# A hybrid decoder trunk on one core: 28 of 76 projection groups as seven products of quarters

## The chip, the core and the metric

One core of a Trainium2 chip runs the whole program in one launch. The metric is device time in microseconds (us). TensorE (PE) multiplies matrices, VectorE (DVE) and ScalarE (ACT) do elementwise work, GpSimd (POOL) a few reductions across partitions, and SyncE (SP) issues most DMAs. "PEld" in the profile is TensorE's loading of a stationary operand.

## What is computed

Two layers. Each normalises its input, projects it to 7,696 columns, sends them through three branches (a gated convolution, stick-breaking attention, gated linear attention or GLA), multiplies each by a SiLU gate, and projects the 2,048 mixed columns back onto the residual. All arrays are float32; there are 512 tokens of width 2,048.

```python
h = rmsnorm(x, norm_g)
proj = h @ w_in                                   # 2048 x 7696
y_conv = cv_b * (conv3(cv_c * cv_h) + bias) * silu(cv_g)
q, k = rmsnorm(sb_q), rmsnorm(sb_k)               # 8 heads of 128
z = q @ k.T / sqrt(128); keep = log_sigmoid(-z)   # strictly causal
w = exp(log_sigmoid(z) + reverse_cumsum(keep) - keep)
y_sb = (w @ sb_v) * silu(sb_g)
y_gla = rmsnorm(gla(gl_q, gl_k, gl_v, decay)) * silu(gl_g)
x = x + concat(y_conv, y_sb, y_gla) @ w_out       # 2048 x 2048
```

## The kernel before

**Float32 by three products.** Every operand of a projection is split into a high and a low float16 part, scaled by powers of two; a product is the sum of high x high, high x low and low x high in PSUM. The input's parts lie transposed in SBUF (`xh`, `xl`: 16 blocks of 128 of the inner dimension by 512 tokens), and so, later, do the parts of the mix (`mh`, `ml`).

**Groups.** The projections are cut into 76 groups of 256 weight columns (GW), 38 a layer, listed in `specs` (L272 to L284): six for GLA (V twice, Q, K, gate twice), four for the first half of the convolution (H, C, gate, B), for each of four head pairs V, gate, Q and K, four for the other half of the convolution, eight for the output. A group comes in three forms:

- `project_cols` (L556): weights stationary, 512 tokens moving; 2 column blocks x 16 x 3 = 96 matmuls. For results wanted with tokens along the free dimension: the convolution, the gates, GLA's q and k.
- `project_toks` (L580): tokens stationary, 256 weight columns moving; 4 token blocks x 16 x 3 = 192 matmuls into two PSUM banks. For V, Q, K of the attention and the output.
- `project_by_token` (L593): the same matmuls, one token block after the other in banks of their own.

PSUM for these results is the pool `psp` with three banks.

**Weights.** `weights()` (L412) opens each group: it fetches the weights two groups ahead from DRAM (`fetch`, two halves on SP's queue) and prepares those one group ahead (`load`, with high priority). Preparation sums the squares of both halves on ScalarE (`wmax`, L319), adds across partitions on GpSimd (L329), makes a power of two of it on VectorE (`wscale`, L330 to L350), then per half the high part on ScalarE (`whi`, L392) and the low part on VectorE (`wlo`, L399). For the output's weights each pair of inner blocks has a scale of its own, since the eight pieces of the mix have different scales (`ratio`, `wparts`).

**Order.** After a start whose VectorE and ScalarE order is written out (L98 to L550), the scheduler orders the instructions of each engine by priority and a timing model; each engine then runs its own in order. GLA's work lies beside the first convolution and head pair 0, attention of a pair beside the next pair's projections: `attend` leaves four pieces in a list, and `go()` emits one behind each projection. In `scores` (L936) a chunk of attention is four ScalarE passes (absolute value, exponential, logarithm, and the positive part), two VectorE passes to combine them, the reverse running sums (L962), a subtraction (L965), an exponential, and the split for the transposing DMAs.

**The mix.** Each finished piece of a branch is scaled and split at once into `mh` and `ml` (`mixsplit`, L643). These tiles also lend space to GLA before their columns are due. At the end of a layer the output groups add the residual (`finish`, L1074); in layer 0 they leave the sum in `xt`, and `xprep` (L472) normalises and splits it for layer 1, one token block at a time during the last group.

## Time and profile before

| | us |
|---|---|
| median of 3 runs | 1742.88 |
| fastest and slowest run | 1742.62, 1743.02 |
| span of the profiled execution, first to last instruction | 1740.9 |
| busy TensorE, VectorE, ScalarE | 1726.8, 1068.9, 1090.0 |

The profile gives its one execution by its span; the runs' times include what lies around a span, about 2.0 us by the median. The rows in the prediction come from these views: the page (busy shares); the timeline (start, duration, engine, line, operation, tiles, shape, count); the chain of work that ended last (start, us, what); the table by stage; and the groups of instructions (line, engine, operation, tiles, shapes, count | busy us, mean ns of one | idle us before them and what ended it). Starts of neighbouring instructions are closer together than durations, since the engines overlap the end of one with the next.

### The profile page before, as it was taken

What the parts mean: (1) busy time and instruction counts of PE and PEld (TensorE: products, weight loads), DVE (VectorE), ACT (ScalarE), POOL (GpSimd) and SP (SyncE); (2) the same over time, 40 slices, a digit from 0 to 9 for tenths busy, and PEclk for the clock granted to TensorE, in tenths of its full rate; (3) what the DMA queues carried; (4) which work ended last, traced back from release to release, by engine and by line L of the source; (5) the groups of instructions that cost most, each with busy time, mean ns of one, the idle gap of its engine ahead of it and who ended that gap; (6) DMA issues with size and microseconds to landing.
All of it is one profiled execution on the core that took longest, in us unless ns stands there. A gap on an engine that the chain in (4) does not pass through costs nothing.

```text
span 1740.9 us, 30651 instructions
## 1 busy us (share of the span) xinstructions
PE 1726.8 (99%) x12846; PEld 1232.4 (71%) x12846; DVE 1068.9 (61%) x2015; ACT 1090.0 (63%) x1460; POOL 75.1 (4%) x104
## 2 busy tenths in 40 slices
PE   8999999999999999999999999999999999999999
PEld 6744556868787754788885455668686868448888
DVE  7556788657665747433474576976575666673431
ACT  7558577667575867455555684766767667663540
POOL 1000000000000000000010000000000000000000
PEclk9999999999999999999999999999999999999999
DMA  6333313335353545444463333133454444453531
GB/s 222 121 97 97 98 58 113 103 104 131 108 140 110 128 121 128 134 158 146 138 148 105 97 97 97 50 121 110 125 124 109 117 124 126 112 132 113 177 124 40
DMA packets 266121, 204.69 MB, mean 118 GB/s; under 512 B 93106, under 2 KB 265212, under 8 KB 265472
## 3 DMA queue, kind: packets, MB, share of 16 engines
q1 hardware_dynamic: 256976, 193.29, 39.0%
q10 hardware_dynamic: 9008, 9.45, 1.6%
q8 instruction: 100, 1.64, 0.4%
q14 instruction: 37, 0.30, 0.1%
HBM read 173.36 MB, written 8.39 MB: 104 GB/s over the span
## 4 chain that ended last, share of the span: by engine, by line
PE 48%; issue 7%; DVE 1%; DMA 1%; SPq 0%; POOL 0%; ACT 0%; POOLq 0%; DVEq 0%
PE psp L576 8%; PE psp L578 8%; PE psp L577 8%; PE psp L570 6%; PE psp L568 6%; PE psp L569 6%; PE psp L601 3%; PE psz L749 1%; PE psm L988 1%; PE psz L944 1%; PE psz L840 0%; DMA m<-raw 0%; DVE wl L399 0%; SPq L487 0%; DMA xs<-x 0%
## 5 line engine op out<-in xcount | busy, mean ns | idle before, releaser
L577 PE MATMUL psp<-wl,m 128*128 128x256 f16 x1664 | 454.0, 273 | 0.0
L578 PE MATMUL psp<-wh,m 128*128 128x256 f16 x1664 | 453.9, 273 | 0.0
L576 PE MATMUL psp<-wh,m 128*128 128x256 f16 x1664 | 453.8, 273 | 0.0
L399 DVE SCALAR_TENSOR_TENSOR wl<-st,ws,wh 128x2048 f16<-128x2048 f32 (+1 forms) x120 | 282.3, 2353 | 193.1 <-ACT wh L392 179.7
L392 ACT ACTIVATE wh<-st,ws 128x2048 f16<-128x2048 f32 (+1 forms) x118 | 236.3, 2003 | 202.6 <-PE psp L569 100.9
L319 ACT ACTIVATE junk<-st 128x2048 uint8<-128x2048 f32 (+1 forms) x150 | 285.5, 1903 | 7.6 <-DMA st<-in_w_out_dram 4.5
L577 PE MATMUL psp<-wl,x 128*128 128x256 f16 x768 | 209.5, 273 | 0.0
L578 PE MATMUL psp<-wh,x 128*128 128x256 f16 x768 | 209.5, 273 | 0.0
L576 PE MATMUL psp<-wh,x 128*128 128x256 f16 x768 | 209.4, 273 | 0.0
L570 PE MATMUL psp<-m,wl 128*128 128x512 f16 x512 | 194.4, 380 | 0.0
L568 PE MATMUL psp<-x,wh 128*128 128x512 f16 x512 | 194.4, 380 | 0.0
L569 PE MATMUL psp<-x,wh 128*128 128x512 f16 x512 | 194.4, 380 | 0.0
L569 PE MATMUL psp<-m,wh 128*128 128x512 f16 x512 | 194.4, 380 | 0.0
L568 PE MATMUL psp<-m,wh 128*128 128x512 f16 x512 | 194.4, 380 | 0.0
L570 PE MATMUL psp<-x,wl 128*128 128x512 f16 x512 | 194.3, 380 | 0.0
L570 PEld LDWEIGHTS <-wl 128*128 128x128 f16 x1024 | 100.1, 98 | 122.8 <-issue 3.7
L569 PEld LDWEIGHTS <-wh 128*128 128x128 f16 x1024 | 100.1, 98 | 117.5 <-issue 1.1
L568 PEld LDWEIGHTS <-wh 128*128 128x128 f16 x1024 | 100.1, 98 | 115.3 <-issue 0.5
L576 PEld LDWEIGHTS <-m 128*128 128x128 f16 x1664 | 162.7, 98 | 19.9 <-issue 0.7
L578 PEld LDWEIGHTS <-m 128*128 128x128 f16 x1664 | 162.6, 98 | 19.4 <-issue 0.5
L577 PEld LDWEIGHTS <-m 128*128 128x128 f16 x1664 | 162.6, 98 | 18.8
L392 ACT ACTIVATE wh<-st,wsr 128x512 f16<-128x512 f32 x128 | 81.6, 710 | 100.5 <-PE psp L578 74.4
(285 smaller groups left out, 2260.4 us busy)
## 6 DMA issues: line engine op xcount, KB each, us to landing
st<-in_w_in_dram SPq DMA_DIRECT2D x120, 1024.0 KB, 5.3
st<-in_w_out_dram SPq DMA_DIRECT2D x32, 1024.0 KB, 5.5
x<-in_x_dram SPq DMA_DIRECT2D x4, 1024.0 KB
qT<-in_x_dram ACTq DMA_DIRECT2D x8, 512.0 KB, 5.3
qT<-xs ACTq DMA_DIRECT2D x8, 512.0 KB
xs<-x SPq DMA_DIRECT2D x14, 256.0 KB, 4.5
out_dram<-kT SPq DMA_DIRECT2D x14, 256.0 KB, 3.7
th<-za SPq DMA_TRANSPOSE x64, 3.6
```

What stands on the lines that cost most here:

```text
L319: S.activation(junk(HK * n).rearrange("p (k n) -> p k n", k=HK), staged[i][h][:, :, :n], AF.Square, accum_out=peak[i][:, h:h + 1])
L392: lasthi[i] = S.activation(wh[:, ks, :n], staged[i][h][:, ks, :n], AF.Copy, scale=s_)
L399: V.scalar_tensor_tensor(wl[:, ks, :n], staged[i][h][:, ks, :n], s_, wh[:, ks, :n], ALU.mult, ALU.subtract)
L568: T.matmul(o, wh[:, kk, cs], xh[:, :, k, :], start=st_, stop=False)
L569: T.matmul(o, wh[:, kk, cs], xl[:, :, k, :], start=False, stop=False)
L570: T.matmul(o, wl[:, kk, cs], xh[:, :, k, :], start=False, stop=en)
L576: T.matmul(o, ah[:, t, k, :], wh[:, kk, :n], start=st_, stop=False, skip_group_check=True)
L577: T.matmul(o, ah[:, t, k, :], wl[:, kk, :n], start=False, stop=False, skip_group_check=True)
L578: T.matmul(o, al[:, t, k, :], wh[:, kk, :n], start=False, stop=en, skip_group_check=True)
L601: T.matmul(o[:, :n], a_[:, t, k, :], w[k // HK][part][:, k % HK, :n], start=i == 0 and k == 0, stop=i == 2 and k == KT - 1)
L749: T.matmul(o, src16[sb][a][:, ss], tgt16[tb][b][:, g0:g1].rearrange("p g h c -> p (g h c)"), start=i == 0, stop=i == 2)
L944: T.matmul(z[:, o:o + (t + 1) * P], qT[:, a_, t, hh, :], kT[:, b_, :t + 1, hh, :], start=i == 0 and o % 512 == 0, stop=False, skip_group_c ...
```

## The change

**Seven products.** A group can be computed as a product of 2 x 2 blocks: tokens in two halves, the inner dimension in two halves, the 256 weight columns in two halves of 128. Instead of eight products of such quarters there are seven, of sums and differences of the quarters, in the form that needs four sums on each side, formed in place. `SEVEN` says which groups: the gate and K of every head pair, H of the second convolution half, output groups 2 to 6; 14 a layer. The sums of the weights are made in `right` for each such group, those of the input once a layer (`x_sums`, right after its preparation), those of the mix once a layer (`mix_sums`, before the output). `seven` runs the products and combines results while they leave PSUM, through `Raw` (to an unscaled SBUF tile) or `Residual` (onto the residual).

**Weights' tiles.** Prepared weights now lie in tiles of a quarter of the inner dimension (six buffers, high and low part together); a normal group uses four, a seven group seven. Stage buffers go from three to four.

**Mix in DRAM.** Finished pieces go to a DRAM tile in float32 (`spill`), and come back during the second convolution half (`mix_load`), except the last four, which are written in place. All pieces get one scale, known after that half's gate; `mix_split` then splits eight pairs, into the same two tiles that held the input's parts. The scale per pair of the output's weights goes. GLA gets tiles of its own.

**Attention and SiLU.** The running sum adds two arrays in one scan, which removes L958 and L965 and turns L959 around. The gate drops two ScalarE passes and replaces one VectorE pass by a minimum.

```diff
+SEVEN = {"gla": (), "conv0": (), "sb": (1, 3), "conv1": (0,), "out": (2, 3, 4, 5, 6)}
...
-    stage = ctx.enter_context(tc.tile_pool(name="stage", bufs=3))
-    wpool = ctx.enter_context(tc.tile_pool(name="wpool", bufs=3))
-    big = ctx.enter_context(tc.tile_pool(name="big", bufs=4))
+    stage = ctx.enter_context(tc.tile_pool(name="stage", bufs=4))
+    wpool = ctx.enter_context(tc.tile_pool(name="wpool", bufs=6))
+    big = ctx.enter_context(tc.tile_pool(name="big", bufs=2))
...
+    def right(i):
+        a, b = (staged[i][0][:, :, c * P:(c + 1) * P] for c in range(2))
+        c, d = (staged[i][1][:, :, c * P:(c + 1) * P] for c in range(2))
+        def part(x):
+            w = wtile(i)
+            hi, lo = (w[:, h, :HK * P].rearrange("p (k n) -> p k n", n=P) for h in range(2))
+            his.setdefault(i, []).append(S.activation(hi, x, AF.Copy, scale=scales[i]))
+            V.scalar_tensor_tensor(lo, x, scales[i], hi, ALU.mult, ALU.subtract)
+        part(a)
+        V.tensor_tensor(b, b, d, ALU.add)
+        V.tensor_tensor(a, a, b, ALU.add)
+        part(a)
+        part(c)
+        V.tensor_tensor(c, c, a, ALU.add)
+        V.tensor_tensor(a, a, d, ALU.subtract)
+        part(a)
+        part(b)
+        part(d)
+        part(c)
...
+    def seven(left, by_cols, evict):
+        w, u = weights()
+        def product(o, n, start, stop):
+            x = left[n]
+            for t in range(1 if by_cols else 2):
+                for k in range(HK):
+                    for i, (xi, wi) in enumerate(((0, 0), (1, 0), (0, 1)) if by_cols else ((0, 0), (0, 1), (1, 0))):
+                        ww = w[n][:, wi, k * P:(k + 1) * P]
...
+                        if by_cols:
+                            T.matmul(o[:, :2 * P], ww, x[xi][:, k, :, :], start=first, stop=final,
+                                     skip_group_check=True)
+                        else:
+                            T.matmul(o[:, t * P:(t + 1) * P], x[xi][:, k, t, :], ww, start=first, stop=final,
+                                     skip_group_check=True)
...
+        ev = evict(u)
+        o1 = bank(psp, "p")
+        product(o1, 0, True, False)
+        with tc.high_priority():
+            s1 = tmp("s1")
+            S.activation(s1, o1[:, :2 * P], AF.Copy, scale=ev.unit)
+        o2 = bank(psp, "p")
+        product(o2, 1, True, True)
+        with tc.high_priority():
+            u2 = tmp("u2")
+            ev.add(u2, o2[:, :2 * P], s1)
+        product(o1, 2, False, True)
+        ev.first(o1[:, :2 * P])
+        o3 = bank(psp, "p")
+        product(o3, 3, True, True)
+        with tc.high_priority():
+            vv = tmp("vv")
+            ev.sub(vv, o3[:, :2 * P], u2)
+        o4 = bank(psp, "p")
+        product(o4, 4, True, False)
+        ev.last4(vv, o4[:, :2 * P])
+        product(o2, 5, True, True)
+        ev.plus(0, 1, o2[:, :2 * P], vv)
+        product(o4, 6, False, True)
+        ev.plus(1, 0, o4[:, :2 * P], u2)
...
+    def column_sums(pieces):
+        tt = V.tensor_tensor
+        for x11, x12, x21, x22 in pieces:
+            tt(x22, x21, x22, ALU.subtract)
+            tt(x21, x11, x21, ALU.subtract)
+            tt(x11, x22, x11, ALU.subtract)
+            tt(x12, x12, x11, ALU.add)
...
+        def mix_split(k, s_):
+            y = m32[k // HK][:, k % HK:k % HK + 2, :]
+            hi, lo = (a[:, k:k + 2].rearrange("p k t c -> p k (t c)") for a in mix)
+            S.activation(hi, y, AF.Copy, scale=s_)
+            V.scalar_tensor_tensor(lo, y, s_, hi, ALU.mult, ALU.subtract)
...
-                S.activation(y, ps[c], AF.Copy, scale=u)
                 a = wk([P, seq], "ga")
-                S.activation(a, y, AF.Abs)
+                S.activation(a, ps[c], AF.Exp, scale=nu)
+                V.tensor_scalar(a, a, 2.0 ** 62, None, ALU.min)
+                S.activation(a, a, AF.Ln, bias=1.0)
                 S.activation(a, a, AF.Exp, scale=-1.0)
-                S.activation(a, a, AF.Ln, bias=1.0)
-                V.scalar_tensor_tensor(a, y, 0.0, a, ALU.min, ALU.subtract)
-                S.activation(a, a, AF.Exp)
-                V.tensor_tensor(y, y, a, ALU.mult)
+                V.scalar_tensor_tensor(g[:, c, :], ps[c], u, a, ALU.mult, ALU.mult)
...
-                    V.scalar_tensor_tensor(w, w, -1.0, a, ALU.mult, ALU.subtract)
-                    V.scalar_tensor_tensor(a, z[:, :zw], zs, w, ALU.mult, ALU.subtract)
...
-                        V.tensor_tensor_scan(back, ones.to_broadcast([P, (t + 1) * P]), back, 0.0,
-                                             ALU.mult, ALU.add)
-                    V.tensor_tensor(w[:, :zw - 1], w[:, :zw - 1], a[:, 1:], ALU.subtract)
+                        V.tensor_tensor_scan(keep_, grow_, keep_, 0.0, ALU.add, ALU.add)
+                    V.scalar_tensor_tensor(w, z[:, :zw], zs, a, ALU.mult, ALU.subtract)
...
+        y = conv_in(1, go)
+        m32 = mix_load()
+        s_ = conv_out(1, y, go)
         while later:
             go()
+        LATE = (10, 11, 2, 3)
+        for k in (0, 4, 6, 8, 12, 14, 10, 2):
+            mix_split(k, s_)
+        if any(modes[cursor[0]:cursor[0] + NG]):
+            sums = mix_sums(s_)
```

`mix_sums` runs `column_sums` twice on 1,024-wide pieces and splits the four sums in eight 1,024-wide steps, ScalarE and VectorE each; `x_sums` does the same on two token blocks of each half, then transposes the parts by sixteen DMAs. `Residual` reads PSUM six times per group and adds in SBUF three times, all 256 wide; `Raw` reads PSUM five times on VectorE. Both also copy the first product out of PSUM on ScalarE, and `Raw` one finished quarter.

533 lines of the change are left out of this document (343 added, 190 removed).

## The prediction

> **What bounds the kernel now.** I first read the page: its head, the busy shares and the granted clock.
>
> ```profile
> span 1740.9 us, 30651 instructions
> PE 1726.8 (99%) x12846; PEld 1232.4 (71%) x12846; DVE 1068.9 (61%) x2015; ACT 1090.0 (63%) x1460; POOL 75.1 (4%) x104
> PEclk9999999999999999999999999999999999999999
> ```
>
> TensorE is busy from end to end at full clock; VectorE and ScalarE are busy six tenths of the time. Since ends of matmuls are modelled, I check the busy share by the distance between starts: rows of the timeline of TensorE, then of the chain of work that ended last.
>
> ```profile
> 1100.18 0.38 PE L568 MATMUL psp<-m,wh 128*128 128x512 f16 x1
> ...
> 1104.28 0.38 PE L569 MATMUL psp<-m,wh 128*128 128x512 f16 x1
> ...
> 1105.20 1.45 PE L749 MATMUL psz<-m 128*128 128x128 f16 x23
> 1106.48 0.38 PE L570 MATMUL psp<-m,wl 128*128 128x512 f16 x1
> ```
>
> ```profile
> 1319.50 0.65 PE psz L944 x3
> ...
> 1410.10 0.65 PE psz L944 x3
> ...
> 1716.33 20.97 PE psp L601 x192
> ```
>
> Between the first two rows lie 19 matmuls of 512 columns: (1104.28 - 1100.18) / 19 = 0.2158 us each. The 23 of 128 columns take (1106.48 - 1105.20) / 23 = 0.0557 us each. The last group has 192 of 256 columns in 20.97 us, 0.1092 us each. So the time of TensorE goes with the columns streamed, with nothing between. One head pair of the attention stage repeats every 1410.10 - 1319.50 = 90.6 us.
>
> The third view is the table by stage (window; its length, then busy time and count of PE, PEld, DVE, ACT, POOL, the clock, DMA share, GB/s).
>
> ```profile
> 0.00:50.00 50.00, 42.33 (x285) 32.19 (x286) 39.05 (x99) 38.93 (x48) 10.24 (x12) 1.00 0.61 200
> 50.00:159.00 109.00, 109.00 (x606) 58.28 (x605) 58.02 (x133) 65.59 (x77) 5.19 (x8) 1.00 0.36 113
> 159.00:255.00 96.00, 96.00 (x553) 48.81 (x551) 75.56 (x153) 64.77 (x105) 1.33 (x3) 1.00 0.24 77
> 255.00:350.00 95.00, 95.00 (x805) 74.81 (x804) 71.85 (x139) 65.69 (x96) 2.62 (x6) 1.00 0.35 106
> 441.00:532.00 91.00, 91.00 (x748) 71.62 (x746) 58.87 (x100) 62.98 (x77) 4.61 (x5) 1.00 0.45 119
> 712.00:754.00 42.00, 42.00 (x388) 37.63 (x387) 14.85 (x32) 15.72 (x32) 0.80 (x2) 1.00 0.35 115
> 754.00:859.00 105.00, 105.00 (x964) 94.00 (x963) 41.69 (x84) 58.21 (x106) 1.99 (x5) 1.00 0.52 164
> 859.00:908.00 49.00, 46.22 (x421) 41.08 (x420) 33.78 (x64) 30.34 (x44) 7.82 (x4) 1.00 0.55 126
> ```
>
> In every stage between the start and the change of layers TensorE leaves nothing idle, so taking columns away shortens each of them, until VectorE, the next engine in the GLA stage (79% and 76%), is full.
>
> **The columns removed.** A column-form group now has 96 matmuls of 512, 96 x 0.2158 = 20.72 us; as seven products it has 7 x 24 = 168 of 256, 168 x 0.1092 = 18.35 us: 2.37 less. A token-form group has 192 of 256, 20.97 us; as seven products 7 x 48 = 336 of 128, 336 x 0.0557 = 18.70 us: 2.27 less. Per layer the table SEVEN makes five column-form groups (four gates, the first of conv1) and nine token-form ones (four K, five of the output). 10 x 2.37 + 18 x 2.27 = **64.5 us** less on the engine that is full. No other matmul changes.
>
> **What it adds to VectorE and ScalarE.** Rows of the groups by line and shape, and of VectorE's timeline, where consecutive instructions overlap a little:
>
> ```profile
> L399 DVE SCALAR_TENSOR_TENSOR wl<-st,ws,wh 128x2048 f16<-128x2048 f32 x116 | 272.4, 2349 | 186.7 <-ACT wh L392 173.2 <-PE psz L946 10.2 <-PE psz L749 2.9
> L392 ACT ACTIVATE wh<-st,ws 128x2048 f16<-128x2048 f32 x114 | 227.9, 1999 | 196.9 <-PE psp L569 100.9 <-PE psp L578 73.9 <-DVE ws L340 9.6
> L1044 DVE TENSOR_TENSOR raw<-raw,qr 128x1024 f32<-128x1024 f32 x8 | 9.8, 1226 | 0.3
> L1053 ACT ACTIVATE qp<-raw 128x1024 f16<-128x1024 f32 x16 | 16.9, 1057 | 44.0 <-DVE raw L1049 25.8 <-DVE raw L1044 18.1
> L330 DVE TENSOR_SCALAR wq<-wgm 128x1 f32<-128x1 f32 x75 | 16.0, 213 | 141.4 <-POOL wgm L329 141.4
> L338 DVE TENSOR_SCALAR wq<-wq 128x1 int32<-128x1 int32 x76 | 11.4, 150 | 1.5
> L735 DVE TENSOR_TENSOR m<-e,m 128x256 f16<-128x256 f32 x32 | 13.4, 423 | 7.8 <-ACT m L734 7.3
> ```
>
> ```profile
> 1267.81 1.20 DVE L620 TENSOR_REDUCE bm<-g 128x1 f32<-128x1024 f32 x1
> 1268.92 2.34 DVE L399 SCALAR_TENSOR_TENSOR wl<-st,ws,wh 128x2048 f16<-128x2048 f32 x1
> 1271.18 1.55 DVE L965 TENSOR_TENSOR zw<-zw,za 128x895 f32<-128x895 f32 x2
> ...
> 1279.12 0.87 DVE L995 SCALAR_TENSOR_TENSOR e<-psm,vu,g 128x256 f32<-128x256 f32 x2
> ```
>
> L399 occupies 1271.18 - 1268.92 = 2.26 us of the engine, 0.09 less than its duration. So a 1024-wide operation costs 1.226 - 0.09 = 1.14 us, a 256-wide one from PSUM about 0.39 (two took 0.87), a 256-wide one in SBUF 0.423 - 0.09 = 0.33.
>
> Preparing a seven group: seven low parts and five sums or differences, each 1024 wide, 12 x 1.14 = 13.7 us of VectorE where two L399 took 4.5 (+9.2), and 7 x 1.06 = 7.4 us of ScalarE where two L392 took 4.0 (+3.4). Its results: five 256-wide operations on VectorE, 2.0 us; the output groups have six from PSUM and three in SBUF, 3.3 us.
>
> *Attention stage, one head pair.* The window 441 to 532 has 58.9 us of VectorE. Two seven groups add 2 x (9.2 + 2.0) = 22.4. Removed are L958, L965 and L648:
>
> ```profile
> L958 DVE SCALAR_TENSOR_TENSOR zw<-zw,za 128x896 f32<-128x896 f32 (+1 forms) x4 | 3.1, 823 | 5.2 <-ACT za L954 5.2
> L965 DVE TENSOR_TENSOR zw<-zw,za 128x895 f32<-128x895 f32 (+1 forms) x4 | 3.1, 812 | 0.0
> L648 DVE SCALAR_TENSOR_TENSOR m<-e,bsmix,m 128x512 f16<-128x512 f32 x2 | 1.5, 752 | 0.0
> L962 DVE TENSOR_TENSOR_SCAN za<-ones,za 128x512 f32<-128x512 f32 (+3 forms) x8 | 5.9, 805 | 0.0
> ```
>
> The first three make 3.1 + 3.1 + 1.5 less ten overlaps of 0.09, 6.8 us. New sum 58.9 + 22.4 - 6.8 = 74.5 us against TensorE's 90.6 - 2.37 - 2.27 = 86.0: 87% full. I cost the scan that adds two arrays like the scan with a constant, L962; the trace has no such scan, and if its second array halved its pace, VectorE would need 5.9 us more and still fit. ScalarE, by these rows:
>
> ```profile
> L611 ACT ACTIVATE g<-psp,wu 128x512 f32<-128x512 f32 x32 | 21.2, 670 | 0.0
> L613 ACT ACTIVATE ga<-g 128x512 f32<-128x512 f32 x32 | 20.0, 630 | 0.5
> L1033 ACT ACTIVATE raw<-psp 128x512 f32<-128x512 f32 x32 | 18.4, 576 | 0.0
> L647 ACT ACTIVATE m<-e,bsmix 128x512 f16<-128x512 f32 x16 | 11.5, 718 | 24.7 <-DVE e L995 24.7
> ```
>
> 63.0 + 2 x 3.4 + some 1.6 for copies of first results, less 2 x (0.67 + 0.63) for the passes that the shorter SiLU drops, 2 x 0.58 for K's raw copies and 2 x 0.72 for the mix: 66 us, 77%. The right-hand sums also make VectorE wait twice per group for a 1.06 us high part of a sum just formed, about 1.1 us each: 4.4 us a head pair, inside the 11.5 idle. So I charge 0 here. The bounds are 0 (other ready work always fills the waits) and 18 groups x 2.2 = 40 us (nothing does); I take 0 because the idle time is more than twice the waits.
>
> *GLA stage into the first head pair.* 75.6 + 71.9 = 147.4 us of VectorE in 191; plus 22.4, less some 4 of mix splits: 166 against 186, 89%. Also 0, inside the same bounds.
>
> *Output stage.* There is no attention work to fill waits. A seven group costs VectorE 13.7 + 3.3 + 0.8 (five scalars of the scale, L330 and four like L338) = 17.8 us against 18.70 of TensorE. With the two waits it is 20.0, so VectorE sets the pace: 1.3 us a group, x 10 = **+13 us**. Below, the bound is 0 (the scheduler pulls two independent high parts forward), above 2.2 x 10 = 22.
>
> *Between attention and output.* The mix is now split at the end: eight pairs at 1.14 = 9.1 us of VectorE, and its sums for the seven products, 8 x 1.14 + 8 x 1.14 = 18.2. The window 712 to 754 has 14.9 us in 42; there the preparation of the first seven group takes the place of eight narrow low parts,
>
> ```profile
> L399 DVE SCALAR_TENSOR_TENSOR wl<-st,wsr,wh 128x512 f16<-128x512 f32 x128 | 87.5, 747 | 40.3 <-ACT wh L392 40.0
> ```
>
> ```profile
> st<-in_w_in_dram SPq DMA_DIRECT2D x120, 1024.0 KB, 5.3
> ```
>
> 13.7 less 8 x 0.66, about 8 more (the second row is the page's, a weight half's fetch and its us to landing). Sum 50 us, in 42 plus what of the last conv group is free (the first half of K is readable there already for overwriting). So VectorE is full for two groups; TensorE needs the sums one product after the other, not at once. I charge 3 us a layer, **+6**; bounds 0 and 50 - 42 = 8 a layer. The twelve loads of the mix from DRAM, 3.1 MB, have about 60 us; with 6.3 MB of weights beside them that is about 155 GB/s, and the start moves 200. Hidden. If it were not, the split would wait, and the output stage with it.
>
> *Layer start.* Sums of the input: 16 x 1.14 = 18.2 us of VectorE and 16 more transposing DMAs, behind the input's preparation, where the window 0 to 50 has 39 of 50 busy and 50 to 159 58 of 109. Seven products don't read them for eleven groups, some 230 us. But if they stand ahead of the evictions of the first two groups, TensorE has three PSUM banks of 5.2 us each, 15.7 us, before it waits. 18.2 plus the low parts of one group, 4.5, less 15.7 is 7 us; the other end is 0. I charge 3 a layer, **+6**.
>
> Moved queues: stores of the mix, its loads and the input's transposes stand on SP before weight fetches. A load waiting for its buffer holds those fetches, but weights are fetched two groups, some 40 us, ahead; cost 0, and the latency of a weight fetch, 5.3 us by the last row above, each time that cover is gone.
>
> **Sum.** On the profiled execution: 1740.9 - 64.5 + 13 + 6 + 6 = 1701.4. The median of the runs is 1742.88, 2.0 above the span; carried along, the forecast is **1703**.
>
> **Rivals.**
>
> 1. *TensorE stays the only bound*: the waits are all filled. Then 1742.9 - 64.5 = 1678. For it: 39% of VectorE is idle before. Against it: it would need the output stage at 95% of VectorE without a bubble.
>
> 2. *Late evictions* (slower). A seven group uses four results in three PSUM banks. The fourth needs the bank of the first; the product that completes the fourth needs its half result read; the next group needs the bank of the second. Each has one product, 48 x 0.0557 = 2.7 us, as cover, and the reading instruction stands in VectorE's queue between the 1.14 us steps of the next weights. Two of these ahead make 2 x 1.14 + 0.39 = 2.7, no wait; three make 3.8, a wait of 1.1. If three stand there at all three places of all 28 groups, that is 3 x 1.1 x 28 = 92 us: 1742.9 - 64.5 + 92 = 1770. It decides above 64.5 / 28 = 2.3 us a group. For it: the engine is 87 to 95% full around these groups, and an engine that waits in order also delays what is behind. Against it: the evictions carry high priority, and two steps are still covered.
>
> 3. *Weight loads bind the 128-column stream.* Each load lasts 98 ns by its row:
>
> ```profile
> L749 PEld LDWEIGHTS <-m 128*128 128x128 f16 x432 | 30.4, 98 | 9.6
> ```
>
> If loads did not overlap one another, 336 x 0.098 = 32.9 us a token-form group instead of 20.97: 1742.9 - 23.7 + 18 x 12.0 = 1935. Against it stands the burst above, 23 loads and matmuls at 0.0557. The row has 432 loads of 98 ns, 42.3 us, in 30.4 us of busy time, so they overlap. The burst is short beside 336 in a row, which no row shows. The Trainium skill, page "TensorE: Matmul & The Clock Gate", section "Back-to-back issue gap", says that a sustained stream of weight load and matmul pairs runs at about 81 ns each at 128 columns. By that, an estimate, a token-form group would take 27.2 us and the kernel 1742.9 - 23.7 + 18 x 6.2 = 1831; the trace disagrees as far as its bursts reach, 55.7 ns.
>
> 4. *The saving is eaten exactly*: the bounds of the attention stage and the others together, 40 + 22 + 16 + 14 = 92, exceed 64.5, so a result near no change can come out, too.
>
> **Chances.** Forecast, some waits filled, 1690 to 1730: 0.50. Rival 1, below 1690: 0.17. More of the bounds, 1730 to 1739: 0.09. Within 0.2%, about what a measurement of this kernel can tell from no change: 0.04. Rival 2: 0.16. Rival 3: 0.04. So faster 0.76, same 0.04, slower 0.20. The range runs from 1680, where every added cost is nearly nothing, to 1748, which takes in rival 4 and the mild end of rival 2; 2 in 10 are left outside, most of it above.
>
> **What will show it.** Step one: matmuls of 128 columns start 56 ns apart in long runs, and TensorE has 64 us less work. Attention: a head pair of 86 us with VectorE near 75 busy; a longer one, with TensorE waiting for high or low weight parts or for PSUM, shows my 0 wrong. Output stage: seven groups of 20 us, VectorE without idle time but for waits on ScalarE's high parts. Mix: a pause of TensorE of about 3 us near the third output group. Start: waits of TensorE for evictions while VectorE forms sums. Rival 2 shows as TensorE's idle time before third and fourth results, put down to VectorE reading PSUM; rival 3 as starts over 80 ns apart without waits. The forecast is wrong if the seven groups last over 21 us, or if the sums take VectorE much longer than 1.14 us a step.

## The result, and the profile after

The changed kernel takes 1766.85 us (median of four runs, 1759.59 to 1770.10) against 1742.95 before on the same chip: 1.0132 times as long, 95% interval 1.0111 to 1.0154. It is slower by 24 us where 40 us less was forecast.

From the page of the kernel after, its head and busy shares, and from its view of cores the mean granted clock:

```profile
span 1768.3 us, 38034 instructions
PE 1694.0 (96%) x16158; PEld 1315.4 (74%) x16158; DVE 1361.6 (77%) x2417; ACT 1188.4 (67%) x1588; POOL 65.3 (4%) x104
...
core 0: 1768.3 us, clock 0.984
```

TensorE has less work and yet the span is longer: its share fell from 99 to 96%, VectorE's rose from 61 to 77%, and the mean clock, 1.00 in every window of before, is 0.984. Part of the 1694.0 is therefore matmuls that ran slowly. The table by stage (length, then busy us of PE, PEld, DVE, ACT, POOL, clock, DMA share, GB/s) says where:

```profile
18.00:63.00 45.00, 34.54 (x249) 28.22 (x249) 42.30 (x82) 32.80 (x44) 1.77 (x4) 0.89 0.51 131
428.00:459.00 31.00, 26.16 (x369) 23.81 (x368) 24.37 (x39) 19.33 (x24) 0.63 (x1) 0.89 0.68 183
459.00:522.00 63.00, 63.00 (x592) 55.84 (x590) 46.48 (x83) 47.31 (x62) 2.69 (x4) 1.00 0.36 91
458.47:554.35 95.88, 89.38 (x960) 79.70 (x958) 71.26 (x122) 66.64 (x86) 3.32 (x5) 0.96 0.50 119
777.00:875.00 98.00, 94.86 (x1682) 94.02 (x1680) 87.41 (x131) 70.37 (x105) 3.61 (x5) 1.00 0.57 180
949.00:984.00 35.00, 27.66 (x109) 11.28 (x107) 14.65 (x27) 14.66 (x19) 4.97 (x4) 0.85 0.75 172
```

Rows one, two and six are the start of layer 0, the group K of head pair 1, and the third group of layer 1: there TensorE idles and its clock is 0.85 to 0.89. Between them (row three, the V, gate and Q groups after that K) it is full at full clock. Row four is one head pair from V to V, row five five seven-product groups of the output.

To add such pauses up, one number is used from here on. The prediction's rows gave the distance between starts of matmuls in a full stream: 0.0557, 0.1092 and 0.2158 us for 128, 256 and 512 columns (and, from the trace of before, 0.1158 and 0.1625 for the few of 272 and 384). The **lost time** of a stretch is the sum over its matmuls of the distance to the next start, less that; it is worked out from the starts in a run's trace. It holds idle time and slow clock together. A group reaches from its first projection matmul to the next group's first, counted in the order of the program.

| lost us | starts of the two layers (six GLA groups each) | K of pairs 1 to 3 and the groups next to it | output | all |
|---|---|---|---|---|
| before | 7.8 | 0 | 0 | 7.5 |
| after | 33.5 | 47.5 | 11.4 | 95.8 |

The rest of the last column, 3.3 us after, lies beside GLA's matmuls in the gate of pair 0. The balance closes: 1740.9 - 64.5 (columns) + 95.8 - 7.5 = 1764.7, and 3.6 is left to the measured 1768.3, at the starts of the layers where other matmuls lie. So the saving is there in full, and 88 us of new pauses eat it.

**One pause at K.** TensorE's timeline after (start, duration, line, tiles, shape, count, idle before and what ended it). L665 are a seven group's products, L626 to L628 the V group that follows, L1199 attention beside them.

```profile
438.03 4.41 PE L665 MATMUL psp<-w,s 128*128 128x128 f16 x76
442.28 0.27 PE L1199 MATMUL psm<-th,v 128*128 128x256 f16 x1
443.86 1.31 PE L1199 MATMUL psm<-th,v 128*128 128x256 f16 x12 [1.31 <-DMA th<-za]
445.01 2.84 PE L665 MATMUL psp<-w,s 128*128 128x128 f16 x48
...
451.25 0.40 PE L626 MATMUL psp<-w,act 128*128 128x256 f16 x1 [3.02 <-DVE wq L356]
...
456.99 0.32 PE L626 MATMUL psp<-w,act 128*128 128x256 f16 x1
```

Three things are in these rows. A wait for transposed attention weights (1.3 us). A wait of 3.0 us before V's first matmul. And behind it 27 matmuls from 451.25 to 456.99, 0.213 us apart where 0.109 is the full pace: half clock, worth 2.8 us more. With a wait of 0.7 us for ScalarE's copy of the first result, ahead of these rows, they make the 8.2 us lost at this K. The Trainium skill, page "TensorE: Matmul & The Clock Gate", section "Part 1: The HAM clock gate", says that the clock falls to half after an idle window of about 3.4 us and knows no steps between; 0.213 against 0.109 agrees with the half, but the wait was 3.02 us, shorter than that window (the last section returns to it).

The second wait is the new one. VectorE's timeline of the same moment:

```profile
442.93 0.42 DVE L709 TENSOR_TENSOR vv<-psp,u 128x256 f32<-128x256 f32 x1
447.11 1.23 DVE L429 TENSOR_TENSOR st<-st,st 128x1024 f32<-128x1024 f32 x1 [3.76 <-DMA st<-in_w_in_dram]
448.25 1.28 DVE L412 SCALAR_TENSOR_TENSOR w<-st,ws,w 128x1024 f16<-128x1024 f32 x1
449.45 1.22 DVE L1266 SCALAR_TENSOR_TENSOR qp<-raw,qp 128x1024 f16<-128x1024 f32 x1
450.58 0.20 DVE L348 TENSOR_SCALAR wq<-wgm 128x1 f32<-128x1 f32 x1
450.77 0.42 DVE L721 TENSOR_TENSOR raw<-psp,vv 128x256 f32<-128x256 f32 x1
```

L721 reads the PSUM bank that V's first matmul needs. Its inputs were there when L709 ended, at 443.3. But VectorE works in order, and ahead of L721 the scheduler had put L429, the first sum of the weights of the gate group of pair 2, which starts at 477.7. L429 waited 3.76 us for those weights to land, and three more steps stood between: the eviction came 7.4 us late. (TensorE's wait is put down to L356, the instruction just behind L721.) Why had the weights not landed? SyncE's queue:

```profile
434.58 0.37 SPq L320 DMA_DIRECT2D st<-in_w_in_dram  x1
435.05 6.23 SPq L1181 DMA_TRANSPOSE th<-za  x3
441.37 0.53 SPq L320 DMA_DIRECT2D st<-in_w_in_dram  x1
```

The first half's fetch (L320) left at 434.58, the second half's only at 441.37, behind three transposes of attention, and L429, which needs both, could start at 447.1. That is still 30 us before the group that multiplies with these weights: they were late for the place of L429 in VectorE's queue, not for TensorE. A fetch also waits until a stage buffer comes free. The largest such wait, after and before (us in all, times, longest):

```profile
SPq L320 <- DVE w L412: 270.4, 30, 20.2
SPq L308 <- DVE wl L399: 975.6, 121, 20.5
```

It is longer before, where nothing is lost at K, so a sum of waits on this queue explains no pause.

L429 stands and waits like this at the K groups of pairs 1 and 2 in both layers, 3.8 to 5.5 us each time. At pair 3 it doesn't, and about 6.6 us are lost each time all the same: TensorE waits for transposed attention weights there, and for an eviction on ScalarE (L713) that stands behind a sum of squares (L332), which itself waited 1.9 us for a fetch.

**The start of layer 0.** VectorE, then TensorE:

```profile
35.65 1.23 DVE L749 TENSOR_TENSOR x<-x 128x1024 f32<-128x1024 f32 x1 [0.66 <-PE psz L498]
...
38.44 1.22 DVE L751 TENSOR_TENSOR x<-x,x 128x1024 f32<-128x1024 f32 x1
39.57 2.48 DVE L488 SCALAR_TENSOR_TENSOR x<-x,xrs,g 128x1024 f32<-128x1024 f32 x2
41.96 2.35 DVE L507 TENSOR_TENSOR act<-psz,act 128x1024 f16<-128x1024 f32 x2
...
43.32 1.94 PE L498 MATMUL psz<-ident,x 128*128 128x128 f32 x8 [5.50 <-DVE act L507]
...
57.14 7.07 PE L638 MATMUL psp<-w,act 128*128 128x272 f16 x47 [4.62 <-ACT w L408]
```

L749 to L751 are sums of the input that nothing reads for eleven groups; they stand ahead of L488 and L507, which prepare the input blocks that TensorE multiplies next.

**The third group of layer 1**, in the timelines of SyncE, ScalarE, VectorE and TensorE:

```profile
956.97 5.51 SPq L775 DMA_TRANSPOSE s<-th  x4
962.58 12.20 SPq L320 DMA_DIRECT2D st<-in_w_in_dram  x3
...
968.20 1.91 ACT L332 ACTIVATE junk<-st 128x2048 uint8<-128x2048 f32 x1 [12.53 <-DMA st<-in_w_in_dram]
...
970.81 0.21 DVE L348 TENSOR_SCALAR wq<-wgm 128x1 f32<-128x1 f32 x1 [14.55 <-POOL wgm L345]
971.13 0.67 DVE L847 COPY e<-psm 16x512 f32<-16x512 f32 x1
...
971.85 2.07 PE L851 MATMUL psm<-e,ga 16*128 16x512 f32 x2 [7.34 <-DVE ws L358]
```

The sixteen transposes of the input's sums (L775) take 5.51 / 4, about 1.4 us of the queue each, 22 us in all. The weight fetch behind them leaves at 962.58, the sum of squares that needs it (L332) waits 12.5 us, and the scale (L348) waits for that. TensorE doesn't need this scale for another 33 us: it is that of the group after next, which starts at 1004.3. What it waits for is the copy L847, which its matmul L851 reads, and L847 stands behind L348 in VectorE's queue. It is the same trap as at K, with another wait at its head. (TensorE's wait is put down to L358, the instruction just behind L847.)

### The profile page after: what moved, and what is told of

Its sections match the earlier page's. It is cut to its first block, busy times and chain, and to the rows that moved or that the text cites. A ratio compares the mean times of both kernels' runs of the same rounds, so it can differ in the third digit from the quotient of the medians.

```text
span 1768.3 us, 38034 instructions
## 1 busy us (share of the span) xinstructions
PE 1694.0 (96%) x16158; PEld 1315.4 (74%) x16158; DVE 1361.6 (77%) x2417; ACT 1188.4 (67%) x1588; POOL 65.3 (4%) x104
## 4 chain that ended last, share of the span: by engine, by line
PE 19%; DVE 14%; issue 12%; DMA 5%; ACT 5%; SPq 1%; POOL 1%; ACTq 0%; DVEq 0%; POOLq 0%
PE psp L665 5%; PE psp L638 2%; PE psp L662 2%; DMA st<-in_w_in_dram 2%; DVE w L412 2%; DVE w L426 2%; PE psp L626 2%; PE psp L628 2%; PE psp L627 2%; ACT junk L332 1%; PE psp L610 1%; PE psp L611 1%; PE psp L612 1%; DMA th<-za 1%; DVE za L1173 1%
## 5 line engine op out<-in xcount | busy, mean ns | idle before, releaser
L626 PE MATMUL psp<-w,act 128*128 128x256 f16 x1280 | 353.7, 276 | 14.9 <-DVE wq L356 11.7
L627 PE MATMUL psp<-w,act 128*128 128x256 f16 x1280 | 353.6, 276 | 0.8 <-DVE w L412 0.8
L628 PE MATMUL psp<-w,act 128*128 128x256 f16 x1280 | 353.2, 276 | 0.0
L332 ACT ACTIVATE junk<-st 128x2048 uint8<-128x2048 f32 x150 | 285.3, 1902 | 53.4 <-DMA st<-in_w_in_dram 52.0
L425 ACT ACTIVATE w<-st,ws 128x1024 f16<-128x1024 f32 x196 | 219.2, 1142 | 150.6 <-DVE st L430 35.4
L412 DVE SCALAR_TENSOR_TENSOR w<-st,ws,w 128x1024 f16<-128x1024 f32 x192 | 244.3, 1279 | 51.6 <-ACT w L408 50.7
L426 DVE SCALAR_TENSOR_TENSOR w<-st,ws,w 128x1024 f16<-128x1024 f32 x196 | 248.3, 1281 | 45.3 <-ACT w L425 43.9
L408 ACT ACTIVATE w<-st,ws 128x1024 f16<-128x1024 f32 x188 | 212.7, 1142 | 90.9 <-PE psp L612 60.0
L610 PE MATMUL psp<-act,w 128*128 128x512 f16 x704 | 268.0, 381 | 0.0
L611 PE MATMUL psp<-act,w 128*128 128x512 f16 x704 | 267.9, 380 | 0.0
L612 PE MATMUL psp<-act,w 128*128 128x512 f16 x704 | 267.7, 380 | 0.0
L662 PEld LDWEIGHTS <-w 128*128 128x128 f16 x1680 | 165.5, 99 | 26.8 <-issue 5.0
L665 PE MATMUL psp<-w,act 128*128 128x128 f16 x2592 | 152.5, 219 | 5.5 <-ACT s L676 4.3
L665 PEld LDWEIGHTS <-act 128*128 128x128 f16 x2592 | 147.4, 98 | 6.9 <-issue 6.4
L638 PE MATMUL psp<-w,act 128*128 128x256 f16 (+1 forms) x1152 | 137.7, 281 | 12.1 <-ACT w L408 5.3
L626 PEld LDWEIGHTS <-act 128*128 128x128 f16 x1280 | 126.9, 99 | 28.4 <-DVE wq L356 12.4
L627 PEld LDWEIGHTS <-act 128*128 128x128 f16 x1280 | 126.9, 99 | 20.0 <-issue 4.1
L628 PEld LDWEIGHTS <-act 128*128 128x128 f16 x1280 | 127.0, 99 | 17.6 <-issue 1.6
L638 PEld LDWEIGHTS <-act 128*128 128x128 f16 x1152 | 114.5, 100 | 33.1 <-issue 9.3
L610 PEld LDWEIGHTS <-w 128*128 128x128 f16 x704 | 69.1, 98 | 82.9 <-issue 3.8
L611 PEld LDWEIGHTS <-w 128*128 128x128 f16 x704 | 69.1, 98 | 82.5 <-issue 3.8
L612 PEld LDWEIGHTS <-w 128*128 128x128 f16 x704 | 69.1, 98 | 82.0 <-issue 2.0
```

The lines of the kernel that those rows point to most:

```text
L332: S.activation(junk(HK * GW).rearrange("p (k n) -> p k n", k=HK), staged[i][h], AF.Square, accum_out=peak[i][:, h:h + 1])
L412: V.scalar_tensor_tensor(lo[:, :, :GW], staged4(i, q), scales[i], hi[:, :, :GW], ALU.mult, ALU.subtract)
L425: his.setdefault(i, []).append(S.activation(hi, x, AF.Copy, scale=scales[i]))
L426: V.scalar_tensor_tensor(lo, x, scales[i], hi, ALU.mult, ALU.subtract)
L610: T.matmul(o, wh, xh[:, k, :, :], start=st_, stop=False)
L611: T.matmul(o, wh, xl[:, k, :, :], start=False, stop=False)
```

## The experiments

Theories, by the letters of the expectations (Q is their name for all these local waits together; B and V, rivals, are explained where they stand). **D**: at the K groups a wait for a weight fetch stands ahead of a pressing eviction. **O**: at the start of a layer the sums of the input stand ahead of the input's own preparation. **S**: the block of sixteen transposes holds up what is behind it on its queue. The rival **R**: the rest of the change (the mix in DRAM, the new tiles, the attention) costs the time, not the seven products.

### Which part

All groups in the ordinary form, the rest of the change kept:

```diff
-SEVEN = {"gla": (), "conv0": (), "sb": (1, 3), "conv1": (0,), "out": (2, 3, 4, 5, 6)}
+SEVEN = {"gla": (), "conv0": (), "sb": (), "conv1": (), "out": ()}
```

> The changed kernel with no seven group at all (the table SEVEN empty): no right-hand sums, no sums of input or mix; the mix in DRAM with one scale, the quarter tiles, the shorter SiLU and the one-scan attention stay. Theory Q (the loss of the changed kernel comes from local waits that the seven groups bring, at the layer starts, beside each K group and at the second output group, lengthened by the halved TensorE clock behind each pause): without them the kernel is bound by TensorE as before, 1743, at most 5 us more. Rival R (the rest of the change costs time by itself, through the mix that returns from DRAM and is split late): 1755 or more.

Measured 1747.44 us, 1.0025 [1.0015, 1.0036] of before, lost time 9.0. The rest of the change costs about 5 us, so R falls. Its profiled run shows 1.6 us of a later first projection (19.70 against 18.10 us) and 0.2 to 0.8 us at each V of pairs 0 and 1.

Only the ten output groups as seven products (`"sb": (), "conv1": ()`):

> Only the output groups 2 to 6 are seven groups; none in the attention and convolution, so no sums of the input either. Theory Q: the ten output groups save 22.7 us and lose about the 10 us of pauses seen in this stage of the changed kernel: about 1731. Rival V (VectorE is too full wherever there are seven groups, so that they last as long as normal ones): 1743 or more.

Measured 1732.85, 0.9942 [0.9927, 0.9957]. Against the run before, 10 x 2.27 = 22.7 us of columns bring 14.6. The lost time of the output is 4.1, and the first group of layer 1, which is prepared beside the last output groups, takes 31.9 us instead of 26.3.

Only the attention's and the convolution's (`"out": ()`):

> Only the seven groups of attention and convolution, normal output groups, so no sums of the mix. Theory Q: all the loss at K groups and layer starts stays and the output's net gain of about 12 goes: 1779. Rival R: less than the changed kernel's 1767, since the sums of the mix are gone.

Measured 1764.72, 1.0126 [1.0102, 1.0150]; lost 29.2 at the starts, 39.6 at K. Three quarters of the loss after are here, and the columns saved, 10 x 2.37 + 8 x 2.27 = 41.9, don't cover it. Theory Q's 1779 is missed by 14 us: the pauses at K are 8 us smaller here than after, and that of layer 1's third group 7. The run doesn't settle the rival's side either, since its four runs (1761 to 1770) lie around the 1767 that it named.

Weight fetches from GpSimd's queue instead of SyncE's, so that they don't stand behind transposes:

```diff
-            nc.sync.dma_start(
+            nc.gpsimd.dma_start(
```

> The changed kernel with the weight fetches issued from GpSimd's queue instead of SP's, so that they stand neither behind transposes nor in front of them. Theory Q in the form that the order on SP's queue makes the pauses: the 10 us at the second group of layer 1 go and most of the 48 us beside the K groups: 1715 to 1730. Rival B (the fetch waits for a stage buffer, held by the sums made in place, whatever queue it is on): only the pause in layer 1 goes, about 1757. Rival V: within 5 us of 1767.

Measured 1809.21, 1.0384 [1.0330, 1.0438]: a miss. The waits of its trace:

```profile
POOL st L320 <- DVE w L412: 511.5, 59, 27.6
...
DVE wq L348 <- POOL wgm L345: 137.8, 49, 12.3
```

The same in-order trap, moved: GpSimd now waits for stage buffers, and the reductions of the weights' scales wait behind it. GpSimd's busy time also rose from 65.3 to 201.6 us, and the first projection began 7 us later. The run doesn't decide about D, as the cure brings a wait of its own; the pause at layer 1's third group did shrink, from 10.3 to 3.3.

### The order at K

D says that L429's place is wrong, not its work. So VectorE's part of the preparation of a seven group's weights is tied behind the last but one PSUM reading of the seven group before it, the one that frees the bank for the next group; the work is the same:

```diff
+            if lastev:
+                with tc.issue_after(lastev.pop().ins):
+                    right(i)
+            else:
+                right(i)
...
-        ev.plus(0, 1, o2[:, :2 * P], vv)
+        made = ev.plus(0, 1, o2[:, :2 * P], vv)
+        lastev[:] = [made]
```

> The changed kernel, with VectorE's share of a seven group's weight preparation issued behind the eviction of the second bank of the seven group before it; nothing else moves. Theory D (beside each K group VectorE, in order, waits for a weight fetch that has not landed, with the eviction that frees TensorE's next bank behind it): the six pauses shrink from 48 us in total to 25 or less, 1745 or less. Rival B (TensorE waits there for the transposed attention weights, and these are late whatever VectorE's order is): within 8 us of 1767.

Measured 1734.06, 0.9951 [0.9936, 0.9966]: 33 us less than after. The loss at K fell from 47.5 to 21.8 and in the output from 11.4 to 2.9; the starts kept 31.6. Its VectorE and TensorE at the same K (L728 is the eviction that was L721):

```profile
448.55 0.42 DVE L728 TENSOR_TENSOR raw<-psp,vv 128x256 f32<-128x256 f32 x1
448.88 1.21 DVE L429 TENSOR_TENSOR st<-st,st 128x1024 f32<-128x1024 f32 x1
...
447.86 0.55 PE L1206 MATMUL psm<-th,v 128*128 128x256 f16 x5 [1.18 <-DMA th<-za]
449.11 0.27 PE L632 MATMUL psp<-w,act 128*128 128x256 f16 x1 [0.70 <-DVE raw L728]
```

The eviction is ahead of L429, and the wait of 3.0 is 0.7. That is D, shown by its cure; but 21.8 of K's 47.5 us stay. TensorE's waits for transposed attention weights fell with it, from 11.7 us in ten to 2.4 in two, so rival B's waits hung largely on the same order.

The input's sums named in the program behind the second group instead of ahead of the first:

```diff
-        sums = x_sums() if any(modes[cursor[0]:cursor[0] + 30]) else None
+        some = any(modes[cursor[0]:cursor[0] + 30])
...
+        sums = x_sums() if some else None
```

> The changed kernel with the sums of the input formed behind the second group of a layer instead of ahead of the first. Theory O (at the layer starts the sums' steps stand in VectorE's order ahead of the input's last low parts and the first evictions): of the 27 us that the layer starts lose over the kernel without seven groups at least 15 come back, 1752 or less; the sixteen transposes still stand ahead of weight fetches on SP and keep the rest. Rival (the sums displace the same work wherever they stand): within 5 us of 1767.

Measured 1768.52, 1.0148 [1.0124, 1.0172], as after. VectorE's timeline of this run:

```profile
35.08 1.22 DVE L749 TENSOR_TENSOR x<-x 128x1024 f32<-128x1024 f32 x1 [0.53 <-PE psz L498]
...
37.74 2.47 DVE L488 SCALAR_TENSOR_TENSOR x<-x,xrs,g 128x1024 f32<-128x1024 f32 x2
```

The scheduler orders by its own model and put the sums back ahead of L488. The edit changed the text, not the order, so it said nothing on O.

Seven products for the gates but not for K, and the other way round (`"sb": (1,)` and `"sb": (3,)`):

> The changed kernel with normal K groups: of the head pairs only the gates are seven groups. Theory D (VectorE's evictions of a seven K group stand behind a wait): the pauses beside the K groups go, eight groups cost 2.27 us more each on TensorE: 1767 - 48 + 18 = 1737. Rival B (attention weights late): half of the pauses stay, 1755 or more.

> The changed kernel with normal gate groups in the head pairs; the K groups stay seven groups. Theory D (the wait that blocks VectorE is that of the next gate's sums for their weights, made in place and fetched late): without those sums the pauses beside K go, eight groups cost 2.37 us more each: 1767 - 48 + 19 = 1738. Rival (K's own preparation fills VectorE): the pauses stay, 1770 or more.

Gates alone: 1734.00, 0.9947 [0.9933, 0.9962], no loss at K at all. K alone: 1743.10, 1.0001 [0.9991, 1.0010], loss at K 3.5; the 1738 expected is missed by 5 us, of which 3.5 are what K still loses. So the pauses need both forms. That K's evictions have no slack and the gate's longer preparation stands ahead of them is our reading of it; no run takes these two apart. The starts lose the same in both, 34.6 and 33.9: they don't depend on which of the two is a seven (without any seven that needs the input's sums, e1 and e2, they lose 6.6 and 8.7).

### The starts of the layers

All four keep the tie of e5. They are, in this order: the sixteen transposes from ScalarE's queue; the input's sums tied behind the last split of the second group; both; both without K's seven products.

```diff
-                        nc.sync.dma_start_transpose(sums[i][hl][:, :, t, :], parts[i, t][:, hl])
+                        S.dma_start_transpose(sums[i][hl][:, :, t, :], parts[i, t][:, hl])
```

```diff
+            with tc.issue_after(ends[0].ins), tc.issue_after(ends[1].ins):
+                sums = x_sums()
```

> The kernel of e5_prep_behind (1734), with the sixteen transposes of the input's sums issued from ScalarE's queue instead of SP's. Theory S (on SP's queue they hold up the weight fetches behind them): the pause in the third group of layer 1, 8 us there, falls below 2: 1727. Rival (transposes and fetches hinder each other in the DMA engines, or ScalarE is held up instead): 1733 or more.

> The kernel of e5_prep_behind (1734), with the input's sums tied behind the last eviction of the second group of a layer on VectorE and on ScalarE (e6_sums_later only named them later; in the order that came of it they stood ahead of the last parts of the input and of the evictions, as before). Theory O (it is their place in VectorE's order ahead of the input's last parts that makes TensorE wait at the start): the 18 us lost in the first two groups of layer 0 fall to 6 or less, 1724 or less, less what the transposes then hold up later. Rival (the same 18 us of VectorE are missing wherever they stand): 1732 or more.

> e5_prep_behind with both edits, transposes on ScalarE's queue and sums behind the second group's evictions. If theories O and S both hold: 1712 to 1720, the remaining loss the 20 us beside the K groups. If only one holds: 1722 to 1728. If neither: 1734.

> e11_both with normal K groups, 20 seven groups in all. The 20 us of pauses beside K go and eight groups cost 2.27 us more each, 18 us: within 4 us of e11_both if nothing else in the attention stage waits; 1710 or less if VectorE's lighter load also ends the pauses in the groups around.

Transposes on ScalarE: 1750.82, 1.0047 [1.0032, 1.0062], worse than e5 by 17 us; the starts lose 49.3. ScalarE and TensorE in layer 1:

```profile
941.36 5.55 ACTq L782 DMA_TRANSPOSE s<-th  x4
946.96 0.94 ACT L836 ACTIVATE v<-psp 128x256 f16<-128x256 f32 x3 [15.04 <-DMA s<-th]
...
948.00 0.38 PE L849 MATMUL psm<-ident,lr 128*16 128x128 f32 x1 [16.77 <-DVE lr L848]
```

The block holds ScalarE as it held SyncE, and there evictions of PSUM (L836) are behind it. Both edits together, 1749.08 (1.0039 [1.0024, 1.0054]), and without K's, 1745.88 (1.0020 [1.0010, 1.0030]), lose 50.2 and 48.5 at the starts for the same reason.

Sums tied: 1724.06, 0.9894 [0.9880, 0.9909], 10 us less than e5. The first two groups of layer 0 lost 18.2 after and 4.7 now: that is O. But a new pause came two groups on, in layer 0's fourth group. GpSimd, VectorE, ScalarE and TensorE there:

```profile
109.50 0.95 POOL L946 MEMSET zw<- 128x1024 f32 x1 [4.53 <-DMA s<-zw]
110.42 0.41 POOL L345 PARTITION_ALL_REDUCE wgm<-wm  x1
...
110.87 0.21 DVE L348 TENSOR_SCALAR wq<-wgm 128x1 f32<-128x1 f32 x1 [5.70 <-POOL wgm L345]
...
112.40 1.26 ACT L904 ACTIVATE qT<-psp,qTs 128x512 f32<-128x512 f32 x2 [5.79 <-DVE qTs L902]
...
113.14 0.59 PE L616 MATMUL psp<-act,w 128*128 128x512 f16 x1 [6.70 <-ACT qT L904]
```

The block of transposes reads its parts from tiles that GLA uses next (`zw` among them). GpSimd's clearing of such a tile waits for the transposes, the reduction of a weight scale waits behind the clearing, VectorE's L348 waits for the reduction with L902 behind it, ScalarE's eviction L904 waits for L902, and TensorE for the bank that L904 reads. S has the culprit right, the block, but not the path: in this run the waits go through GpSimd and the tiles, not through a late fetch. The four expectations: e9 came out on its rival's side, e11 outside all its three cases, e12 within the 4 us of e11 that it gave, and e10 at its limit of 1724.

### The block halved

The sixteen transposes as two blocks of eight: the column sums and two of the four sums behind the second group, the other two behind the fourth, GLA's own tiles after that. Traffic and work are the same.

```diff
-        for i in (0, 2, 1, 3):
+        for i in pair:
...
+            with tc.issue_after(ends[0].ins), tc.issue_after(ends[1].ins):
+                sums = x_sums(0)
...
+            with tc.issue_after(enda.ins), tc.issue_after(endv.ins):
+                sums.update(x_sums(1))
```

It was run with K's seven products and without; between them e10 without K's.

> e10_sums_behind (1724) with the sixteen transposes in two blocks of eight: two of the four sums of the input behind the second group, two behind the fourth. Theory S (one block holds its queue for some 20 us, so that the weight fetches behind it land late and an engine in order waits for them with evictions behind): the pause of 9 and 7 us in the fourth group shrinks to 3 or less in each layer, 1712. Rival (what hinders is the transposes' traffic itself): about the same total pause, spread over two groups, 1721 or more.

> e10_sums_behind with normal K groups, 20 seven groups in all. Theory D (the rest of the pauses beside K, 18 us, comes with the K groups' own evictions): these go, eight groups cost 2.27 us more: 1724, within 3. Rival (attention's transposes are late by themselves): the pauses stay in part, 1730 or more.

> e13_two_blocks with normal K groups. If both theories hold, within 3 us of e13_two_blocks; below it by more if VectorE's lighter load also helps elsewhere.

Measured 1707.33 (0.9800 [0.9786, 0.9815]), 1720.29 (0.9873 [0.9858, 0.9888]) and **1704.28** (0.9780 [0.9764, 0.9797]), which beats both kernels. From the page of the two-block kernel with K:

```profile
span 1705.6 us, 38026 instructions
PE 1669.7 (98%) x16158; PEld 1304.5 (76%) x16158; DVE 1359.3 (80%) x2417; ACT 1186.3 (70%) x1588; POOL 65.7 (4%) x104
```

TensorE and VectorE have the matmuls and operations of the kernel after (x16158, x2417); yet 24.3 us of TensorE's busy time are gone, with the slow clock: the mean clock is 1.000 here. The starts lose 7.9, as much as before the change. Block and order changed together, though: the clearing of `zw`, at 109.50 in e10 in the middle of the transposes, comes at 118.18 here, behind those that it must wait for. No run halves the block without that, so the size of the block alone is not shown to be the cause. The rival falls, as the traffic is the same and the pauses are gone. The run came out 5 us below the 1712 expected, e14 4 below its 1724, and e15 3 below this one.

| lost us | starts | K | output | all | median us |
|---|---|---|---|---|---|
| after | 33.5 | 47.5 | 11.4 | 95.8 | 1766.85 |
| e5, preparation behind eviction | 31.6 | 21.8 | 2.9 | 60.1 | 1734.06 |
| e7, gates only | 34.6 | 0 | 3.5 | 41.9 | 1734.00 |
| e9, transposes on ScalarE | 49.3 | 19.2 | 3.8 | 76.7 | 1750.82 |
| e10, sums behind as well | 24.4 | 19.8 | 3.4 | 51.0 | 1724.06 |
| e13, in two blocks | 7.9 | 20.0 | 3.5 | 35.1 | 1707.33 |
| e14, e10 without K | 21.8 | 0 | 2.9 | 29.0 | 1720.29 |
| e15, e13 without K | 7.2 | 0 | 2.9 | 13.2 | 1704.28 |

What is left at K with everything in order, 20 us, is about what K's products save (8 x 2.27 = 18.2): with or without them the kernel takes the same to 4 us (e10 and e14, e13 and e15).

## Why the prediction was wrong

**TensorE's columns, -64.5: right.** In the 76 matmuls between 438.03 and 442.28 of the first pause shown, the distance is 4.25 / 76 = 0.0559 us. Whole output groups of 336 take 18.76 us, 0.0558 each. That also ends rival 3: loads don't bind a long stream of 128 columns. The 81 ns that the Trainium skill, page "TensorE: Matmul & The Clock Gate", section "Back-to-back issue gap", gives don't occur in these streams.

**VectorE and ScalarE, head pair: right in size.** 74.5 and 66 us were forecast; the window of 95.88 us has 71.26 and 66.64. Less the 9.90 us lost in it, the pair takes 86.0, the forecast number. A low part of 1024 took 1.28 us and a high part 1.14 where 1.226 and 1.057 were assumed from rows of other operations.

**Output stage, +13: too high.** The ten seven groups lose 5.3 us after (18.8 to 20.5 us each, 20.0 forecast), 3 with the order mended. The pauses of the second output group, 6.2 us, match the **6 of the mix**, but by luck: TensorE waits there for VectorE's readings of PSUM (3.3 us in two, in layer 1 with half clock behind), the pauses are gone in e5, where the work is the same, and did not occur in e2. Order makes them, not a full VectorE.

**"Attention stage … I charge 0": the step that failed**, by 47.5 us. Its argument, idle time more than twice the waits, compares sums. The engine had the idle time (VectorE was 24.37 of 31.00 us busy around that K), but a wait does not fill it when the next instruction in the queue is one that waits. What decides is which instruction stands ahead of the eviction and what it waits for.

**"Moved queues … cost 0" failed beside it.** It asked whether weights land before TensorE needs them, and they did, some 30 us ahead at the pause shown. What it left out is who waits for them earlier: the first sum in VectorE's queue, 3.76 us, with an eviction behind it. The transposes of attention ahead of the fetch on SyncE's queue lengthen that wait; the price named, 5.3 us "each time that cover is gone", has the size of the four waits (3.8 to 5.5), for another reason.

**"Layer start +6": mis-sized**; 25.7 us more were lost there than before. It foresaw the sums ahead of evictions in the first two groups (18.2 us lost in layer 0, 4.7 with the sums tied behind) but priced only VectorE's time. The sixteen transposes were listed as an addition and not followed on their queue: 22 us of SyncE, with fetches behind them, and behind these fetches a scale in VectorE's queue ahead of a copy that TensorE needs.

**Clock taken as full: failed.** It fell to half behind the long pauses, all six of K's among them; at the K shown that is 2.8 us more after a wait of 3.0.

**Rival 2** (late evictions, 1770) had the right side and nearly the number, by the wrong arithmetic: three short waits in all 28 groups. What happened is fewer and deeper: six of the eight K groups, 6.6 to 9.9 us each. At four of them the queue ahead of the eviction held a wait for a fetch besides three steps; at the other two the eviction on ScalarE was late. Gates, convolution and most output groups are nearly untouched. So the number was luck.

**The forecast of 1703** stands close to the mended kernels' 1707 and 1704, and that is luck as well. It charged 25 us: 13 and 6 at the output, 6 at the starts, 0 at K. The two-block kernel loses 27.6 us more than before, elsewhere: 20 at K, 3.5 at the output, nothing more at the starts. The one without K's seven products saves 18 us of columns less and loses 20 at K less.

**Open:** why K still loses 20 us in e5, e10 and e13. It isn't the slow clock: in e13 the clock is full at every K, in e5 it halves behind one of the six. In e13 TensorE's waits over the whole kernel name VectorE's reading of K's third result (L716, 6.7 us in four), ScalarE's copy of a first result (L682, 4.1 in five) and transposed attention weights (L1214, 3.9 in three). The first of these is the place that rival 2 named. With ordinary gates (e8) K loses only 3.5, so these waits, too, seem to need the gate's preparation beside K. No run took them apart.

## What to carry to other kernels

When a change adds work to an engine that is not the bound, don't ask only whether it has room: for each result that the bound engine needs soon, list what stands ahead of it in every in-order queue, and whether any of that waits for something needed later. Preparation ahead of time must be tied behind the evictions of the moment, and a block of DMAs must be followed through its own queue, the tiles it reads and whoever writes them next. This change, slower by 24 us as it stood, was faster by 35 with the same work in another order.

## What the runs showed of the hardware

- Transposing DMAs of 128 x 1024 float16 hold the queue that issues them about 1.4 us each (5.55 / 4), on ScalarE's queue as on SyncE's, and the engine's other instructions wait with it: 15 us in e9.
- The granted clock changes by stretches of 3.41 us, and waits within one stretch add up. In every run all its changes lie whole multiples of 3.41 us apart. In e5 the waits behind the K shown are 1.18 and 0.70 us, with 0.55 us of work between, and the matmuls from 449.98 to 453.16 still start 0.21 us apart. By window, as in the table by stage:

```profile
446.58:449.99 3.41, 1.52 (x16) 1.16 (x14) 3.41 (x4) 2.85 (x5) 0.40 (x1) 1.00 0.89 274
449.99:453.40 3.41, 3.41 (x19) 2.43 (x17) 2.48 (x10) 1.59 (x2) 0.37 (x1) 0.50 1.05 238
```

A stretch with 1.52 us of TensorE's work is followed by one at half clock; TensorE is busy all through that one, and the next has full clock again. After the pause of the kernel after, the half clock lasts two stretches, 450.24 to 457.07, behind one with 1.41 us of work. The runs show no sharp limit: in e3 a stretch with 1.45 us of work (449.44 to 452.85) kept full clock. The Trainium skill's page "TensorE: Matmul & The Clock Gate", section "Part 1: The HAM clock gate", speaks of an idle window of about 3.4 us; the length agrees, but here less idle time in it was enough.
- Issuing 152 DMAs of 1 MB took GpSimd 136 us of busy time (201.6 against 65.3 us), some 0.9 us each.
